# Hybrid SSM/attention layer with 32 experts: the mix product by column halves, earlier loads of x and the norm rows, and the b_down product moved to the 19th expert

## The chip, the cores and the metric

The kernel runs on one core of one Trainium2 chip. The metric is the device time in microseconds of one launch, as the median of several runs. The engines are named as in the profile: PE (TensorE, matrix products; PEld its weight loads), DVE (VectorE), ACT (ScalarE), POOL (GpSimd) and SP (SyncE, which here only issues DMAs). Each engine works through its own instructions in the order in which the program has them; semaphores make one wait for another.

## What is computed

One decoder layer for 256 tokens of width 1024, all in float32:

```python
proj   = x @ w_in                      # -> z, xBC, dt, q, k, v, gates
y_ssm  = mamba2_branch(z, xBC, dt) @ w_ssm_out       # 2048 x 1024
y_attn = sliding_window_attention(q, k, v) @ w_attn_out  # 1024 x 1024
merged = sigmoid(g0) * y_ssm + sigmoid(g1) * y_attn
h      = layer_norm(alpha * x + merged @ w_mix_out)
top_logits, top_idx = top_k(h @ w_router + b_router, 4)   # of 32 experts
gate_w = softmax(top_logits)
y_e    = swiglu(h @ w_gate_up[e] + b_gate_up[e]) @ w_down[e] + b_down[e]
out    = layer_norm(alpha * h + sum over the 4 of gate_w * y_e)
```

An expert's weights are 1024 x 2048 (gate/up) and 1024 x 1024 (down), 12 MiB; all 32 are read, 403 MB.

## The kernel before the change

**Front.** The weights of the front (w_in, w_attn_out, w_ssm_out, w_mix_out) come as a stream of 50 pieces of 1 MiB. SP loads piece i into one half of a pair of tiles, `ring`, which alternates (prefetch_raw, L101); a half is free again when piece i - 2 has been split. A split (split_ahead, L160) makes two fp32r tiles of a piece: ACT copies it (the high parts, L65), DVE subtracts the copy from it (the low parts, L68). A product then takes three matmuls in place of one: high by high, high by low, low by high (mm3, L332; mix, L826). Splits are made `la` pieces ahead; la is 1 here. Pieces 34 to 37 are w_attn_out (tile `ya`), 38 to 45 w_ssm_out (`yss`), 46 to 49 w_mix_out (`mix`). "Split 37" below is the split of piece 37, tile `w37` in the rows of the program's order.

**The pool.** `gran` has ten blocks of 16 KiB per partition. The ring, each split, large intermediate tiles (the attention output, the gated SSM output yt, the gates, the merged product m) and each piece of expert weights take one. A new tile is given a block when the program is built, and its first writer waits for the last user of the tile that had it.

**Attention and SSM product** (L762 to L819). Four steps of two 24-matmul groups on `ya`, then eight groups of 48 on `yss`, two for each of four output slices. Between them, PE turns the gated SSM output (L676), and ACT and DVE split what was turned. `later` and `run_due` put DVE and ACT work behind the group whose result it takes: for the SSM product a merge (mg, mrg, m: L782) with the gates. The loads of x, the two rows of the first norm, the router's weights (wr) and bias (br) are issued in the third of the four SSM steps (mix_loads, L789).

**Mix, norm, router** (L929 to L957). The mix product has two halves of tokens, c, and two of columns, and each half of columns takes two of the four pieces: mix(c, q). Before the change, c = 0 goes through all four q, then c = 1. resid adds x and takes the statistics of a half of columns; first_norm finishes a half of tokens; turn transposes it, logits multiplies it with the router, top finds the top four on DVE, place counts positions within each expert, one_hot makes the matrix that gathers an expert's tokens.

**Experts.** The work is a list of slots: for expert e eight "u" slots (gate/up) and then four "d" slots (down) of expert e - 1. Each block of 2 MiB serves two slots; SP issues block m when `prefetch` (L118) is reached for it in the program's order, in the mix and later up to nine blocks ahead of the slot (AH). `at(n, f)` puts f at slot n. residual(c) puts alpha * h into the accumulators `out` by a product with a scaled identity; residual(0) stands in the top-4 wait, residual(1) at slot 1. gates_down (L965) at slot 4 counts rows per expert, transposes the gate weights and has GpSimd load b_down; bias_down (L980) at slot 6 adds gate_w times b_down to the accumulators.

Of the kernel before, what the change touches and what calls it, by code (L numbers as in the profile page):

```python
# [8 lines left out]
F = mybir.dt.float32  # L9
# [6 lines left out]
P = 128  # L16
D = 1024
NT = 256
# [12 lines left out]
EXP_TANH = "exp_and_others"  # L31
SILU = "silu_and_others"
OVER, AL = 27, 7
DT, DD = 2, 4
D3 = 4
L1 = 1
# [7 lines left out]
def hybrid_layer(ctx, tc, x, w_in, conv_w, conv_b, dt_bias, a_log, d_skip, norm_w, w_ssm_out,  # L44
                 sinks, w_attn_out, b_gates, w_mix, ln1_g, ln1_b, w_router, b_router,
                 w_gate_up, b_gate_up, w_down, b_down, ln2_g, ln2_b, out, cap=CAP):
    nc = tc.nc
# [9 lines left out]
    def pair(name, dt=F):  # L57
        t = ptile(name, dt)
        return t[:, 0:2048], t[:, 2048:4096]

    def bank(name):
        return psum.tile([P, 512], F, name=name, tag="bank")

    def act(o, i, func=AF.Copy, **kw):
        return nc.scalar.activation(o, i, func, **kw)  # L65
# [12 lines left out]
    def mm(o, l, r, start, stop):  # L78
        return nc.tensor.matmul(o, l, r, start=start, stop=stop)  # L79

    def rows(ap, n, off=0):
        return bass.AP(tensor=ap.tensor, offset=ap.offset + off, ap=[[0, P], [1, n]])
# [5 lines left out]
    stream = []  # L88
# [9 lines left out]
    single = lone.tile([P, 2048], F, name="single")  # L98
    ring = pair("ring")

    def prefetch_raw():  # L101

        while st["dma"] < S_E:
            i = st["dma"]
            ap, nb = stream[i]
            if i - 2 >= st["split"]:
                break
            t = ring[i % 2]
            t3 = t.rearrange("p (k n) -> p k n", n=nb)
            nk = 2048 // nb // len(halves(i))  # L110
            for k in range(len(halves(i))):
                nc.sync.dma_start(t3[:, k * nk:k * nk + nk], ap[:, k * nk:k * nk + nk])
            raws[i] = t
            st["dma"] += 1

    moe = [0]

    def prefetch(upto):  # L118

        while moe[0] < min(upto, len(stream) - S_E):  # L120
            m = moe[0]
            ap, nb = stream[S_E + m]
            t = ptile(f"w{m}").rearrange("p (k n) -> p k n", n=nb)
            last = S_E + m == len(stream) - 1
            for ks in (slice(0, 2), slice(2, 3), slice(3, 4)) if last else (slice(0, 4096 // nb),):
                nc.sync.dma_start(t[:, ks], ap[:, ks])
            raws[S_E + m] = t
            moe[0] += 1

    def halves(i):  # L130

        return [slice(0, 1024), slice(1024, 2048)] if i == 0 else [slice(0, 2048)]
# [6 lines left out]
    def run_due():  # L139
        for t in sorted(t for t in due if t <= clock[0]):  # L140
            for fn in due.pop(t):
                fn()
# [72 lines left out]
    def w1(shape, name, dt=F):  # L215
        return work.tile(shape, dt, name=name, tag="w1", bufs=TB["w1"])
# [4 lines left out]
    def w4(shape, name):  # L221
        return work.tile(shape, F, name=name, tag="w4", bufs=TB["w4"])
# [119 lines left out]
    def take():  # L342
        nxt[0] += 1
        w = weights(nxt[0] - 1)
        if pend[0]:
            pend[0] = False
            side()
        return w
# [410 lines left out]
    bgn = bgn[0:32]  # L759
    nc.sync.dma_start(bgn, b_gate_up[0])  # L760
    mrg = mrg.rearrange("p (b t) -> p b t", t=NT)
    for n in range(4):  # L762
        hi, lo = take()
        for b in range(2):
            ps = bank(f"ya{n}{b}")[:, 0:NT]
            mm3(ps, hi, lo, slice(b * P, (b + 1) * P), att["h"], att["l"])
            later(1, lambda ps=ps, blk=2 * n + b: stt(mrg[:, blk], gts[1][:, blk], 1.0, ps, OP.add, OP.mult))
            tick(b == 1)
# [17 lines left out]
        act(mh[:, blk], mrg[:, blk], scale=0.5)  # L786
        stt(ml[:, blk], mrg[:, blk], 0.5, mh[:, blk].bitcast(F), OP.mult, OP.subtract)

    def mix_loads():  # L789
        xr = single.rearrange("p (c d) -> p c d", d=D)  # L790
        nc.sync.dma_start(xr, x[0].rearrange("(c p) d -> p c d", p=P))
        lnc = [w4([P, D], n) for n in ("lng", "lnb")]
        nc.sync.dma_start(lnc[0], rows(ln1_g, D))
        nc.sync.dma_start(lnc[1], rows(ln1_b, D))
        wr3 = w1([P, 8, 32], "wr")
        nc.sync.dma_start(wr3, w_router[0].rearrange("(k p) e -> p k e", p=P))
        br = w1([P, 32], "br")
        nc.sync.dma_start(br, rows(b_router, 32))
        return xr, lnc, wr3, br

    st["la"] = LS
    for n in range(4):
        prefetch((0, 1, 2, 2)[n])
        if n == 1:
            nc.scalar.preload_act_table_set(EXP_LN)
        if n == 2:
            xr, lnc, wr3, br = mix_loads()
        ps = [bank(f"yss{n}{b}")[:, 0:NT] for b in range(2)]
        for kh in range(2):
            hi, lo = take()  # L810
            if n == 3 and kh == 1:
                prefetch(3)
            for b in range(2):
                mm3(ps[b], hi, lo, slice(b * P, (b + 1) * P), *yT[kh], kh == 0, kh == 1)
                if kh:
                    later(1, lambda b=b, n=n, ps=ps: merge(2 * n + b, ps[b]))
                tick(b == 1)
            if n == 0 and kh == 0:
                bias_cols()  # L819
# [6 lines left out]
    def mix(c, q):  # L826
        hf, kh = divmod(q, 2)
        while len(wm) <= q:
            wm.append(take())
        hi, lo = wm[q]  # L830
        cs = slice(c * P, (c + 1) * P)
        for k in range(4):
            kk = 4 * kh + k
            mm(pm[c][hf], mh[:, kk, cs], hi[:, k], kk == 0, False)
            mm(pm[c][hf], mh[:, kk, cs], lo[:, k], False, False)
            mm(pm[c][hf], ml[:, kk, cs], hi[:, k], False, kk == 7)
# [3 lines left out]
    def resid(c, hf):  # L840
        hs = slice(512 * hf, 512 * hf + 512)
        stt(xr[:, c, hs], xr[:, c, hs], ALPHA, pm[c][hf], OP.mult, OP.add)
        nc.vector.bn_stats(bst[:, c, hf], xr[:, c, hs])
# [44 lines left out]
    def logits(c):  # L888
        pl[c] = bank(f"lg{c}")[:, 0:32]
        for k in range(8):  # L890
            mm(pl[c], hT[c][:, k], wr3[:, k], k == 0, k == 7)

    def top(c):
        tt(lg[:, c], pl[c], br, OP.add)
        nc.vector.max(t8[:, c], lg[:, c])
        ts(nm[:, c:c + 1], t8[:, c, 0:1], -1.0, None, OP.mult)
        nc.vector.memset(t8[:, c, 4:8], 3.0e38)
        nc.vector.match_replace(rp[:, c], t8[:, c], lg[:, c], -3.0e38)
        ts(mk[:, c], rp[:, c], -2.9e38, None, OP.is_le)
# [2 lines left out]
    G2 = const.tile([P, 2, 2, 64], F, name="G2")  # L902

    def place(c):
        if c:
            mm(pp[:, 1], ones, mk[:, 0], True, False)
        mm(pp[:, c], slt, mk[:, c], c == 0, True)
        stt(posm[:, c], pp[:, c], 1.0, mk[:, c], OP.add, OP.mult)
        ts(posm[:, c], posm[:, c], -1.0, None, OP.add)
# [10 lines left out]
    def residual(c):  # L920
        for hf in range(2):
            po[c][hf] = bank(f"out{c}{hf}")
            hs = slice(512 * hf, 512 * hf + 512)
            mm(po[c][hf], ia, hn[:, c, hs], True, False)

    def first_norm(c):
        norm(hn[:, c], [xr[:, c, 0:512], xr[:, c, 512:1024]], bst[:, c].rearrange("p a b -> p (a b)"), lnc, f"l1{c}")

    for q in range(4):  # L929
        mix(0, q)  # L930
        if q % 2:
            resid(0, q // 2)
        if q == 0:
            prefetch(4)
    mix(1, 0)
    first_norm(0)
    prefetch(5)
    mix(1, 1)
    resid(1, 0)
    prefetch(6)  # L940
    mix(1, 2)
    prefetch(7)
    mix(1, 3)
    resid(1, 1)
    prefetch(10)
# [6 lines left out]
    place(0)  # L952
    one_hot(0, 0)
    logits(1)
    top(1)
    place(1)
    one_hot(0, 1)  # L957
# [4 lines left out]

    gwT, bd = [], []

    def gates_down():  # L965

        mm(pp[:, 2], ones, mk[:, 0], True, False)
        mm(pp[:, 2], ones, mk[:, 1], False, True)
        nc.vector.tensor_reduce(cnt, pp[0:1, 2], op=OP.max, axis=AX.X)
        nc.vector.tensor_copy(cnti, cnt)  # L970
        pgt = bank("gwT")
        for c in range(2):
            nc.tensor.transpose(pgt[0:32, c * P:(c + 1) * P], gw[:, c], ident)
        gwT.append(mo.tile([P, NT], F, name="S", bufs=2))
        for hf in range(2):
            bd.append(mo.tile([P, 512], F, name="y", bufs=2))
            nc.gpsimd.dma_start(bd[hf][0:32], b_down[0, :, 512 * hf:512 * hf + 512])
        at(5, lambda: act(gwT[0][0:32], pgt[0:32, 0:NT]))

    def bias_down():  # L980
        for c in range(2):
            for hf in range(2):
                mm(po[c][hf], gwT[0][0:32, c * P:(c + 1) * P], bd[hf][0:32], False, False)

    front.close()

# [7 lines left out]
    def at(n, fn, pre=True):  # L994
        events.setdefault((n, pre), []).append(fn)
# [190 lines left out]

    gather(None, 0)
    at(0, lambda: (soft(0), soft(1), nc.scalar.preload_act_table_set(SILU)), pre=False)
    at(1, lambda: residual(1), pre=False)
    at(4, gates_down, pre=False)  # L1190
    at(6, bias_down, pre=False)
    cur = None
    for n, (kind, e, kp) in enumerate(slots):
        fire(n, True)
# [73 lines left out]
```

## Time and profile before

| | |
|---|---|
| median of 3 runs | 1339.33 us (1338.72 to 1339.79) |
| the profiled execution | 1339.34 us, its span 1337.6 us |
| mean granted TensorE clock | 0.98 |
| PE busy | 1252.5 us (94%) |
| DVE, ACT busy | 431.6 us (32%), 282.9 us (21%) |
| read from HBM | 461.11 MB, 346 GB/s over the span |

Times in the profile are microseconds from the first instruction. A row of the time line has start, duration, engine, line, operation, tiles (out<-in), shape, count, and in brackets how long the engine had stood and what ended that. A row of windows has the stretch, its length, then busy time and number of instructions for PE, PEld, DVE, ACT, POOL, then the granted clock, the share of the DMA engines and GB/s. A row of waits has the total, the number and the longest. A DMA issue row has count, size and the median time from issue to landing. A float32 product or a large one shows as two matmul records.

### The profile page before, as it was taken

The numbers are of one execution on the slowest core, as the hardware profiler recorded it, in microseconds if no ns is written. First come the engines' busy times: TensorE is split into PE (matmuls) and PEld (weight loads), VectorE is DVE, ScalarE is ACT, GpSimd is POOL, SyncE is SP. The second block draws the span as 40 slices with busy tenths as digits, with TensorE's granted clock in tenths as the row PEclk, the third lists the DMA queues.
The fourth block names the chain that finished last, engine by engine and source line by source line (L and its number), as shares of the span: only waits on it lengthen the run. The fifth ranks groups of instructions, "written<-read, shape, count | busy, mean of one in ns | idle before, by whom it ended". The sixth has DMA issues, their size and how long they took to land. (4 is left out here: it accounts for less than half of the span.)

```text
span 1337.6 us, 16127 instructions
## 1 busy us (share of the span) xinstructions
PE 1252.5 (94%) x6864; PEld 682.1 (51%) x6864; DVE 431.6 (32%) x816; ACT 282.9 (21%) x477; POOL 66.4 (5%) x37
## 2 busy tenths in 40 slices
PE   7998999999879999999999999898999999879985
PEld 7997878999754443433434434232333333233321
DVE  5999876565551211111121111111111121111113
ACT  4555545543311101100111011010101101001001
POOL 0045314000000000000000000000000000000000
PEclk9999989999988999999999999999999999989998
DMA  7543334657888999999999999999999999999994
GB/s 227 159 126 97 121 99 126 189 166 238 319 342 335 383 429 431 431 431 430 430 430 430 430 430 431 430 430 431 430 431 431 431 431 430 431 427 430 430 430 172
DMA packets 78741, 463.30 MB, mean 346 GB/s; under 512 B 6908, under 2 KB 45956, under 8 KB 53924
## 3 DMA queue, kind: packets, MB, share of 16 engines
q1 hardware_dynamic: 78452, 460.99, 84.6%
q8 instruction: 57, 0.93, 0.3%
q10 hardware_dynamic: 144, 1.05, 0.2%
q14 instruction: 24, 0.20, 0.0%
q0 software_dynamic: 64, 0.13, 0.0%
HBM read 461.11 MB, written 1.05 MB: 346 GB/s over the span
## 5 line engine op out<-in xcount | busy, mean ns | idle before, releaser
L79 PE MATMUL u<-w,xg 128*64 128x512 f32 x2048 | 464.5, 598 | 22.1 <-DMA w<-in_w_gate_up_dram 22.1
L79 PEld LDWEIGHTS u<-w,xg 128*64 128x64 f32 x2048 | 140.2, 137 | 314.7 <-issue 263.5
L79 PE MATMUL d<-w,ac 128*64 128x512 f32 x1024 | 241.1, 602 | 19.7 <-DVE gg L73 10.3
L1032 DVE COPY gu<-u 128x512 f32<-128x512 f32 x32 | 22.1, 691 | 682.9 <-PE u L79 682.9
L79 PE MATMUL ws<-x,w 128*128 128x256 f32 x1200 | 154.9, 289 | 2.8 <-ACT w L65 2.5
L79 PEld LDWEIGHTS ws<-x,w 128*128 128x128 f32 x1200 | 149.3, 195 | 6.1 <-ACT w L65 2.8
L79 PEld LDWEIGHTS d<-w,ac 128*64 128x64 f32 x1024 | 68.5, 137 | 142.3 <-issue 125.1
L68 DVE TENSOR_TENSOR w<-ring,w 128x2048 fp32r<-128x2048 f32 (+1 forms) x51 | 119.6, 2349 | 25.9 <-ACT w L65 25.7
L65 ACT ACTIVATE w<-ring 128x2048 fp32r<-128x2048 f32 (+1 forms) x51 | 95.8, 1878 | 76.0 <-DMA ring<-in_w_ssm_out_dram 13.1
L65 ACT ACTIVATE gu<-u 128x512 f32<-128x512 f32 x32 | 19.1, 597 | 318.3 <-PE u L79 318.3
L79 PEld LDWEIGHTS xg<-G,single 128*128 128x128 f32 x512 | 64.3, 200 | 24.9 <-issue 24.3
L79 PE MATMUL xg<-G,single 128*128 128x128 f32 x512 | 70.5, 292 | 0.2 <-DVE G L68 0.2
L79 PE MATMUL out<-y,S 64*128 64x512 f32 (+1 forms) x264 | 67.6, 616 | 0.8 <-ACT y L65 0.8
L65 ACT ACTIVATE xg<-xg 128x512 f32<-128x512 f32 x32 | 19.1, 597 | 219.5 <-PE xg L79 219.5
L65 ACT ACTIVATE hg<-hg 128x512 f32<-128x512 f32 x32 | 20.2, 631 | 153.0 <-DVE hg L72 153.0
L79 PE MATMUL yss<-yt,w 128*128 128x256 f32 x384 | 48.3, 288 | 4.0 <-ACT w L65 3.6
L79 PE MATMUL z<-w,x 128*128 128x512 f32 x192 | 50.3, 414 | 0.0
L79 PEld LDWEIGHTS yss<-yt,w 128*128 128x128 f32 x384 | 47.5, 196 | 4.6 <-ACT w L65 3.9
L1043 PEld LDWEIGHTS tu<-ident,gu 128*128 128x128 f32 x256 | 33.4, 210 | 26.3 <-issue 25.2
L79 PEld LDWEIGHTS out<-y,S 64*128 64x128 f32 (+1 forms) x264 | 23.4, 186 | 44.1 <-issue 42.5
L68 DVE TENSOR_TENSOR hg<-tu,bgu 128x256 f32<-128x256 f32 x64 | 26.8, 419 | 49.2 <-PE tu L1043 49.1
L79 PEld LDWEIGHTS z<-w,x 128*128 128x128 f32 x192 | 36.9, 196 | 10.1 <-issue 2.0
(213 smaller groups left out, 835.2 us busy)
## 6 DMA issues: line engine op xcount, KB each, us to landing
w<-in_w_gate_up_dram SPq DMA_DIRECT2D x128, 2048.0 KB, 38.4
w<-in_w_down_dram SPq DMA_DIRECT2D x63, 2048.0 KB, 38.8
ring<-in_w_in_dram SPq DMA_DIRECT2D x33, 1024.0 KB, 5.1
ring<-in_w_ssm_out_dram SPq DMA_DIRECT2D x8, 1024.0 KB, 5.3
ring<-in_w_attn_out_dram SPq DMA_DIRECT2D x4, 1024.0 KB, 5.1
ring<-in_w_mix_out_dram SPq DMA_DIRECT2D x4, 1024.0 KB, 7.2
single<-in_x_dram SPq DMA_DIRECT2D x2, 512.0 KB, 3.7
ring<-in_w_in_dram SPq DMA_DIRECT2D x2, 512.0 KB, 7.7
```

Of the source, the lines that this page charges most:

```text
L65: return nc.scalar.activation(o, i, func, **kw)
L68: return nc.vector.tensor_tensor(o, a, b, op=op)
L79: return nc.tensor.matmul(o, l, r, start=start, stop=stop)
L1032: nc.vector.tensor_copy(t, banks[hf])
L1043: nc.tensor.transpose(pb[:, b], gu[hf][:, b:b + 509:4], ident)
```

## The change

- **Loads.** x, norm rows, wr and br are issued ahead of the attention product, not in the SSM product. At its second step the last two pieces of w_mix_out (48 and 49) are loaded into a second ring pair (load_early), at the third step expert block 0 (prefetch(1)). Expert blocks 1 and on are issued from the mix on.
- **Splits.** When the SSM product is through, its last merge is put out, and then the splits of all w_mix_out pieces that remain (47 to 49).
- **Mix by column halves.** Both halves of tokens take columns 0 to 511 (pieces 46, 47), then both the rest (48, 49). first_norm(0) stands behind mix(1, 2).
- **Top-4 wait.** The count product `pos<-mk,ones` is taken out of place, and residual(1) is put between it and the second top-4.
- **b_down.** Slot 4 only counts rows. b_down is loaded as one tile 40 slots ahead of slot 220, the gates are transposed at slot 220, in the block of the 19th expert, and multiplied at slot 222.

```diff
+BIAS = 12 * 18 + 4
...
+    def load_early(*idx):
+        for i, t in zip(idx, pair("ring")):
+            early[i] = t
+            load_raw(i, t)
...
     nc.sync.dma_start(bgn, b_gate_up[0])
     mrg = mrg.rearrange("p (b t) -> p b t", t=NT)
+    xr = single.rearrange("p (c d) -> p c d", d=D)
+    nc.sync.dma_start(xr, x[0].rearrange("(c p) d -> p c d", p=P))
+    lnc = [w4([P, D], n) for n in ("lng", "lnb")]
+    nc.sync.dma_start(lnc[0], rows(ln1_g, D))
+    nc.sync.dma_start(lnc[1], rows(ln1_b, D))
+    wr3 = w1([P, 8, 32], "wr")
+    nc.sync.dma_start(wr3, w_router[0].rearrange("(k p) e -> p k e", p=P))
+    br = w1([P, 32], "br")
+    nc.sync.dma_start(br, rows(b_router, 32))
     for n in range(4):
+        if n == 1:
+            load_early(S_MIX + 2, S_MIX + 3)
+        if n == 2:
+            prefetch(1)
         hi, lo = take()
...
     for n in range(4):
-        prefetch((0, 1, 2, 2)[n])
         if n == 1:
             nc.scalar.preload_act_table_set(EXP_LN)
-        if n == 2:
-            xr, lnc, wr3, br = mix_loads()
...
             if n == 3 and kh == 1:
-                prefetch(3)
+                st["la"] = 2
...
     def place(c):
-        if c:
-            mm(pp[:, 1], ones, mk[:, 0], True, False)
         mm(pp[:, c], slt, mk[:, c], c == 0, True)
...
-    for q in range(4):
-        mix(0, q)
-        if q % 2:
-            resid(0, q // 2)
-        if q == 0:
-            prefetch(4)
+    run_due()
+    st["la"] = 4
+    split_ahead(S_MIX)
+    prefetch(3)
+    mix(0, 0)
+    prefetch(4)
+    mix(0, 1)
+    resid(0, 0)
+    prefetch(5)
     mix(1, 0)
-    first_norm(0)
-    prefetch(5)
+    prefetch(6)
     mix(1, 1)
     resid(1, 0)
-    prefetch(6)
+    prefetch(7)
+    mix(0, 2)
+    mix(0, 3)
+    resid(0, 1)
     mix(1, 2)
-    prefetch(7)
+    first_norm(0)
     mix(1, 3)
     resid(1, 1)
     prefetch(10)
...
     logits(1)
+    mm(pp[:, 1], ones, mk[:, 0], True, False)
+    residual(1)
     top(1)
...
-    at(1, lambda: residual(1), pre=False)
-    at(4, gates_down, pre=False)
-    at(6, bias_down, pre=False)
+    at(4, count_rows, pre=False)
+    at(BIAS - 40, load_bd, pre=False)
+    at(BIAS, lambda: gates_turned(BIAS), pre=False)
+    at(BIAS + 2, bias_down, pre=False)
```

How this moves instructions shows at three places. In the rows, numbers behind a name tell buffers apart; "waits" names the semaphores an instruction waits for, by the engine (or DMA queue) that raises them. The first is ACT in the attention product before the change: w36 to w38 are the copies of pieces 36 to 38, yt2 the turned SSM output.

```order
L65 ACTIVATE w36_2855<-ring_70 128x2048 [waits DMAHW0_49,DVE_49]
L65 ACTIVATE yt2_2799<-yt20_2860 128x4x128 [waits DVE_49,PE_49,Activation_49]
L65 ACTIVATE w37_2925<-ring_70 128x2048 [waits DMAHW5_49,DMAHW2_49,DVE_49]
L65 ACTIVATE yt2_2799<-yt21_2893 128x4x128 [waits PE_49]
L65 ACTIVATE w38_2988<-ring_70 128x2048 [waits DMAHW3_49,PE_49,Activation_49]
```

And the same place with the change:

```order
L66 ACTIVATE w36_2867<-ring_70 128x2048 [waits DVE_49,DMAHW0_49,PE_49,Activation_49]
L66 ACTIVATE yt2_2808<-yt20_2872 128x4x128 [waits DVE_49,PE_49,Activation_49]
L66 ACTIVATE w37_2939<-ring_70 128x2048 [waits DMAHW7_49,DVE_49,PE_49]
L66 ACTIVATE yt2_2808<-yt21_2905 128x4x128
L66 ACTIVATE w38_3002<-ring_70 128x2048 [waits DMAHW2_49,DVE_49,PE_49]
```

The order is the same, but the copies w36 and w37 now wait for PE too: w36 has the block of split 34, w37 that of split 36, and the semaphore count in the program is that of the last matmul that reads them.

The second place is PE from the mix to the first expert before the change: ht is the transposed h, lg the logits, pos the positions, xg the gathered tokens, u the gate/up product.

```order
L79 MATMUL mix00_3550<-w47_3569,m_3054 128x512 x12
L79 MATMUL mix01_3551<-w48_3592,m_3054 128x512 x12
L79 MATMUL mix01_3551<-w49_3609,m_3054 128x512 x12
L79 MATMUL mix10_3552<-w46_3491,m_3054 128x512 x12
...
L79 MATMUL pos_3567<-mk_3560,ones_3558 128x32
L79 MATMUL pos_3567<-mk_3560,slt_105 128x32
L79 MATMUL xg00_3815<-G2_3568,single_69 128x128 x8
```

With the change:

```order
L80 MATMUL mix00_3548<-w47_3572,m_3068 128x512 x12
L80 MATMUL mix10_3550<-w46_3492,m_3068 128x512 x12
L80 MATMUL mix10_3550<-w47_3572,m_3068 128x512 x12
L80 MATMUL mix01_3549<-w48_3574,m_3068 128x512 x12
...
L80 MATMUL pos_3565<-mk_3558,ones_3556 128x32
L80 MATMUL out10_3796<-single_69,ia_3555 128x512
L80 MATMUL out11_3798<-single_69,ia_3555 128x512
L80 MATMUL pos_3565<-mk_3558,slt_105 128x32
L80 MATMUL xg00_3820<-G2_3566,single_69 128x128 x8
```

The product of the second half of tokens with the first half of columns (mix10) stood behind all four groups of the first half of tokens, and now stands behind the first two of them; the residual product of the second half of tokens (out10, out11) has come in front of the second half's count product.

The third place is SP, which issues the loads, from the attention pieces on; before the change:

```order
L760 DMA mrg_2785<-in_b_gate_up_dram 32x2048
L112 DMA ring_70<-in_w_attn_out_dram 128x8x256
L112 DMA ring_70<-in_w_ssm_out_dram 128x8x256 x5
L126 DMA w0_3186<-in_w_gate_up_dram 128x4096
L112 DMA ring_70<-in_w_ssm_out_dram 128x8x256 x2
L126 DMA w1_3305<-in_w_gate_up_dram 128x4096
L791 DMA single_69<-in_x_dram 128x2x1024
L793 DMA lng_3308<-in_ln1_g_dram 128x1024
L794 DMA lnb_3309<-in_ln1_b_dram 128x1024
L796 DMA wr_3312<-in_w_router_dram 128x8x32
L798 DMA br_3314<-in_b_router_dram 128x32
L112 DMA ring_70<-in_w_ssm_out_dram 128x8x256
```

With the change:

```order
L771 DMA mrg_2785<-in_b_gate_up_dram 32x2048
L774 DMA single_69<-in_x_dram 128x2x1024
L776 DMA lng_2788<-in_ln1_g_dram 128x1024
L777 DMA lnb_2789<-in_ln1_b_dram 128x1024
L779 DMA wr_2792<-in_w_router_dram 128x8x32
L781 DMA br_2794<-in_b_router_dram 128x32
L109 DMA ring_70<-in_w_attn_out_dram 128x8x256
L109 DMA ring_2864<-in_w_mix_out_dram 128x4x512 x2
L109 DMA ring_70<-in_w_ssm_out_dram 128x8x256
L137 DMA w0_2937<-in_w_gate_up_dram 128x4096
L109 DMA ring_70<-in_w_ssm_out_dram 128x8x256 x7
L109 DMA ring_70<-in_w_mix_out_dram 128x4x512 x2
```

The five small loads stand ahead of the last attention piece, two mix pieces ahead of the first SSM piece, expert block 0 (here w0) behind that; block 1 has left this stretch.

More of the change, by code (lines that the diff above doesn't have):

```diff
@@ L99, in hybrid_layer, with load_raw @@
     ring = pair("ring")
+    early = {}
+    def load_raw(i, t):
+        ap, nb = stream[i]
+        t3 = t.rearrange("p (k n) -> p k n", n=nb)
+        nk = 2048 // nb // len(halves(i))
+        for k in range(len(halves(i))):
+            nc.sync.dma_start(t3[:, k * nk:k * nk + nk], ap[:, k * nk:k * nk + nk])
+        raws[i] = t
     def prefetch_raw():
@@ L104, in prefetch_raw @@
             i = st["dma"]
[L105 to L113, printed above, removed]
+            if i not in early:
+                if i - 2 >= st["split"]:
+                    break
+                load_raw(i, ring[i % 2])
             st["dma"] += 1
+    def load_early(*idx):
+        for i, t in zip(idx, pair("ring")):
+            early[i] = t
+            load_raw(i, t)
     moe = [0]
@@ L787, in merge @@
         stt(ml[:, blk], mrg[:, blk], 0.5, mh[:, blk].bitcast(F), OP.mult, OP.subtract)
[L789 to L799, printed above, removed]
     st["la"] = LS
     for n in range(4):
-        prefetch((0, 1, 2, 2)[n])
         if n == 1:
             nc.scalar.preload_act_table_set(EXP_LN)
-        if n == 2:
-            xr, lnc, wr3, br = mix_loads()
         ps = [bank(f"yss{n}{b}")[:, 0:NT] for b in range(2)]
@@ L963, in hybrid_layer, with count_rows @@
     gwT, bd = [], []
-    def gates_down():
+    def count_rows():
         mm(pp[:, 2], ones, mk[:, 0], True, False)
@@ L970, in gates_down, with load_bd, gates_turned @@
         nc.vector.tensor_copy(cnti, cnt)
+    def load_bd():
+        bd.append(mo.tile([32, D], F, name="bd", bufs=1))
+        nc.gpsimd.dma_start(bd[0], b_down[0])
+    def gates_turned(n):
         pgt = bank("gwT")
@@ L974, in gates_down @@
         gwT.append(mo.tile([P, NT], F, name="S", bufs=2))
[L975 to L978, printed above, removed]
+        at(n + 1, lambda: act(gwT[0][0:32], pgt[0:32, 0:NT]))
     def bias_down():
@@ L982, in bias_down @@
             for hf in range(2):
-                mm(po[c][hf], gwT[0][0:32, c * P:(c + 1) * P], bd[hf][0:32], False, False)
+                mm(po[c][hf], gwT[0][0:32, c * P:(c + 1) * P], bd[0][:, 512 * hf:512 * hf + 512], False, False)
     front.close()
```

## The prediction

> **What bounds the kernel now.** I read the page first, then the waits of the DMA-issuing queue, the windows around the start of the experts, and the instructions of TensorE in order of time from 280 to 470 us. The profiled execution took 1339.34 us: a span of 1337.6 and 1.74 around it. The median of the three runs is 1339.33, so no correction is needed between the two; 0.2%, 2.7 us, is about what a measurement can tell from no change.
>
> ```profile
> span 1337.6 us, 16127 instructions
> 404.90:460.20 55.30, 54.59 (x254) 25.21 (x256) 10.33 (x36) 7.30 (x13) 1.16 (x2) 0.92 0.90 344
> 460.20:1312.00 851.80, 809.97 (x3880) 309.02 (x3877) 125.73 (x330) 84.91 (x150) 0.30 (x1) 1.00 1.01 430
> ```
>
> The last three columns are granted clock, busy share of the DMA engines and GB/s. From 460 to 1312 us the expert weights arrive at 430 GB/s with the DMA engines full: a block of 2 MiB every 4.88 us, and nothing on an engine shortens that. What can move the end is the moment at which this stream becomes unbroken. In the 55 us before it ran at 344 GB/s, while TensorE was busy 54.59 of 55.30.
>
> ```profile
> SPq L126 <- PE u L79: 55.7, 8, 20.4
> 415.60 0.33 SPq L126 DMA_DIRECT2D w<-in_w_gate_up_dram  x1
> w<-in_w_gate_up_dram SPq DMA_DIRECT2D x1, 2048.0 KB, 7.8
> 450.40 0.33 SPq L126 DMA_DIRECT2D w<-in_w_gate_up_dram  x1
> w<-in_w_gate_up_dram SPq DMA_DIRECT2D x1, 2048.0 KB, 9.8
> ```
>
> The first row is of 410 to 460 us: the queue that issues expert blocks waits for the gate/up products to free a block. The pool holds ten, so block 10 goes out only when the products on block 0 end (415.60; it lands 7.8 us later), and block 16 at 450.40, landing at 460.2. From there on the stream is unbroken. So the end of the kernel hangs on when TensorE reaches the first expert, and on how fast it frees blocks 0 to 6. Both are sums over TensorE, below.
>
> ```profile
> 298.19 3.12 PE L79 MATMUL ya<-att,w 128*128 128x256 f32 x24
> 301.50 6.00 PE L79 MATMUL ya<-att,w 128*128 128x256 f32 x48
> 315.22 34.81 PE L79 MATMUL yss<-yt,w 128*128 128x256 f32 x288
> 353.68 2.57 PE L79 MATMUL yss<-yt,w 128*128 128x256 f32 x16 [3.65 <-ACT w L65]
> 356.65 4.96 PE L79 MATMUL yss<-yt,w 128*128 128x256 f32 x32 [0.40 <-DVE w L68]
> 361.44 3.13 PE L79 MATMUL mix<-w,m 128*128 128x512 f32 x13
> 366.74 5.58 PE L79 MATMUL mix<-w,m 128*128 128x512 f32 x23 [2.16 <-DVE w L68]
> 376.72 0.79 PE L79 MATMUL mix<-w,m 128*128 128x512 f32 x1 [4.40 <-ACT w L65]
> 379.05 15.31 PE L79 MATMUL mix<-w,m 128*128 128x512 f32 x59 [1.53 <-DVE w L68]
> 351.72 1.91 ACT L65 ACTIVATE w<-ring 128x2048 fp32r<-128x2048 f32 x1 [7.64 <-DMA ring<-in_w_ssm_out_dram]
> 333.06 11.51 SPq L798 DMA_DIRECT2D br<-in_b_router_dram  x1
> ```
>
> **Part by part: SSM product.** TensorE's 3.65 us wait stems from the x and norm loads: the last of them, br, held the issuing queue for 11.51 us, and the next weight piece left behind it, so that its copy waited until 351.72. The change sends these loads 50 us earlier. The wait goes, and with it the half-clock stretch that followed. Without both, the last 48 products take a sixth of the 34.81 us, 5.8, in place of 11.4 (350.03 to 361.44): 5.6 us off.
>
> **Attention product.** The loads land here, where a weight piece of 1 MiB is used every 6.0 us (48 products); what they cost DMA is hidden by that. But two blocks of the pool are now taken early (the second ring, expert block 0). The order of ScalarE shows split 37 waiting for TensorE: its block is that of split 36, free when the products on 36 end, 298.19 + 3.12 = 301.31.
>
> ```profile
> L65 ACT ACTIVATE w<-ring x20: 1901/1914/1918, 249.4 to 374.8; 128x2048 fp32r<-128x2048 f32 x20
> L68 DVE TENSOR_TENSOR w<-ring,w x20: 2281/2284/2293, 251.4 to 376.7; 128x2048 fp32r<-128x2048 f32 x20
> 301.78 0.60 ACT L65 ACTIVATE yt<-yt 128x512 fp32r<-128x512 f32 x1 [2.08 <-PE yt L676]
> 296.99 0.69 DVE L68 TENSOR_TENSOR yt<-yt,yt 128x512 fp32r<-128x512 f32 x1 [2.46 <-ACT yt L65]
> 361.65 0.42 DVE L76 SCALAR_TENSOR_TENSOR mg<-gate,yss 128x256 f32<-128x256 f32 x1 [0.82 <-PE yss L79]
> 362.10 0.42 DVE L68 TENSOR_TENSOR mrg<-mrg,mg 128x256 f32<-128x256 f32 x1
> ring<-in_w_attn_out_dram SPq DMA_DIRECT2D x4, 1024.0 KB, 5.1
> ring<-in_w_ssm_out_dram SPq DMA_DIRECT2D x1, 1024.0 KB, 6.9
> ```
>
> A copy takes 1.91 us, so the high parts come at 303.2 instead of 301.50: 1.7 us of standing. The low parts come later still: queued behind the copy is the turned piece yt on ScalarE (0.60), behind that its subtraction (0.69) and a merge (0.42) on VectorE, then the subtraction of the split, 2.28: 4.0 us, in which TensorE has 16 products of 0.125 us (48 in 6.00), 2.0. Another 2.0. I add 3.7; at best the second stall overlaps and it is 1.7, at worst a late piece adds the 1.8 by which the landing of the piece behind br (6.9 us, the last row) passes the median of the attention pieces.
>
> **Mix.** Now 32.9 us, 361.44 to 394.36. A product costs 0.24 us (13 in 3.13, 23 in 5.58), so 96 take 23.1; the rest is waiting for pieces that had not landed or not been split, and the clock. All four pieces are now in the chip by then. What is late next: the copy of the second piece stands on ScalarE behind the last merge. After the last SSM product come 0.2 us, two VectorE steps of 0.42, a copy of 0.42, then 1.91 and 2.28: low parts at 5.7 us, while TensorE has 13 products, 3.1. A stall of 2.6; the third and fourth splits are ready at 8.0 and 10.3, before they are used. 25.7 instead of 32.9: 7.2 off.
>
> **Clock.**
>
> ```profile
> 355.20:358.70 3.50, 3.10 (x15) 2.81 (x14) 3.50 (x2) 1.17 (x1) 0.00 (x0) 0.51 0.18 22
> 375.70:382.50 6.80, 4.24 (x9) 3.06 (x10) 2.29 (x1) 0.97 (x1) 0.00 (x0) 0.50 0.63 213
> 403.00:409.80 6.80, 5.77 (x26) 5.34 (x26) 1.66 (x10) 0.00 (x0) 1.16 (x2) 0.50 1.01 431
> 430.30:433.70 3.40, 3.40 (x10) 0.85 (x10) 0.00 (x0) 0.60 (x1) 0.00 (x0) 0.50 0.93 390
> ```
>
> Four stretches at half clock, two of 3.4 us and two of 6.8: one after the 3.65 us wait, one after 4.40, one in the top-4 wait, and one at 430 with TensorE busy 3.40 of 3.40. New stalls of about 2 us lie between; I count one stretch of 3.4, 1.7 us lost, with 0 and 3.4 as ends. The Trainium skill, "TensorE: Matmul & The Clock Gate" (Part 1), has the clock fall only after about 3.4 us of idling; by it this term would be 0 and the forecast 1.7 lower. The stretch at 430, with no idling in it, speaks against that.
>
> **Top-4 wait and first expert.**
>
> ```profile
> 403.96 0.61 PE L79 MATMUL pos<-mk,ones 128*128 128x32 f32 x2
> 405.37 0.64 PE L79 MATMUL pos<-mk,slt 128*128 128x32 f32 x2 [0.79 <-DVE mk L72]
> 411.90 3.65 PE L79 MATMUL u<-w,xg 128*64 128x512 f32 x16
> 415.49 1.98 PE L79 MATMUL out<-single,ia 128*128 128x512 f32 x4
> 423.17 0.38 PE L973 MATMUL gwT<-ident,gw 128*32 128x128 f32 x2
> 427.06 4.00 PE L79 MATMUL out<-y,S 32*128 32x512 f32 x8
> 431.00 4.99 PE L79 MATMUL u<-w,xg 128*64 128x512 f32 x16
> ```
>
> The residual product (1.98) now starts at about 404.5 and ends at 406.5; the count product behind it started at 405.37, so 1.1 is added (up to 3.1 if all of it runs at half clock). The first norm, moved a product later, ends about with the mix; 0.4 for that. Together 1.5. In return the first expert loses 1.98, about 0.3 (turning the gates), 4.0 (b_down), and the half clock in the 16 products at 431 (4.99 against 3.65: 1.3): 7.6 off.
>
> Sum. First expert product: 3.7 - 5.6 - 7.2 + 1.7 + 1.5 = 5.9 earlier, 406.0. Blocks from 3 on are freed 5.9 + 7.6 = 13.5 earlier. Block 10 goes out at 406.0 + 3.7 = 409.7 and lands at 417.5; blocks 1 to 9, issued as the mix proceeds from about 360, need 9 x 4.88 = 44 us and are in by about 406, so they don't bind. From 417.5 the stream can run at 4.88: block 16 would land at 446.8, and its issue (450.4 - 13.5 = 436.9, with 9.8 to land) allows it. I add 1.0, since with only two blocks under way the stream ran below 430 GB/s in the first window. 447.8 against 460.2: 12.4 earlier, and every later block with it.
>
> **b_down at the 19th expert.**
>
> ```profile
> PE u L79 <- DMA w<-in_w_gate_up_dram: 19.9, 23, 2.0
> w<-in_w_gate_up_dram SPq DMA_DIRECT2D x128, 2048.0 KB, 38.4
> ```
>
> The first row is of 600 to 1190 us: TensorE waits for weights about once an expert, so 4.3 us (6 with a half-clock stretch) are made up within some six experts. Until then the stream has 38.4 us of issued blocks: 0. Without that cover the 4.3 to 6 would be lost. The b_down load is as large as before.
>
> 1339.3 - 12.4 = 1326.9.
>
> **The rivals.**
> A: the new stalls do not halve the clock, the second attention stall overlaps: 3.4 less, 1323.5. For it: 2.16 us of waiting at 364.6 cost no clock. 0.18.
> B: the front gains nothing, only the first expert's 7.6 counts: 1339.3 - 7.6 + 1.0 = 1332.7. It needs 5.9 us more of waiting in the attention and SSM products: x, the norm rows and the router's 1024 rows of 128 bytes, behind which br held the queue for 11.51 us, now stand ahead of the last attention piece and the first SSM pieces. Against it: no product uses those pieces before 301, 20 us after the loads start. 0.17.
> C, slower: in the SSM product each split needs the block of the split two before, and the ring slot of the load two before: copy 1.91, subtraction 2.28, some 1.5 of queueing, load, within two groups of products, 11.6 us. A landing of up to about 5.9 us fits. At 10.3 each of four rounds loses 4.4, 17.6 in all: 1344.5. It decides from a landing of about 9.0 on, where four rounds eat the 12.4. Against it: after block 0 nothing else is in that queue. 0.03.
> D: no change: the blocks themselves come too late for an earlier stream. Blocks 1 to 16 would have to take from 362 to 460, 6.1 us each; that is the 344 GB/s of the first window, but there the queue was waiting for free blocks. 0.03.
>
> **Numbers.** The forecast (1324.5 to 1330) has 0.57; D and C 0.03 each; the 0.02 left are larger gains. The unknown terms (attention -2 to +1.8, clock +-1.7, count product +2, up to 5 us if the stream stays below 430 GB/s up to block 16) reach from 1322 to 1335; I give 1321.5 to 1334. Faster by over 0.2%: 0.94; within: 0.03; slower: 0.03.
>
> **What would show it.** Right: no wait behind br near 350; two waits of about 2 us near 301 to 307; a mix of about 26 us with one wait of 2 to 3; first expert product near 406; block 16 landing near 448, then 430 GB/s; no new wait of the issuing queue near the 19th expert. Wrong: a first expert product after 410, or gaps in the stream after 450.

## The result, and the profile after

The changed kernel takes 1324.48 us (median of 4 runs, 1324.27 to 1324.78) against 1339.28 for the kernel before in the same comparison: 14.8 us less, ratio 0.989 (95% interval 0.9873 to 0.9907). The forecast was 1326.9 with a range of 1321.5 to 1334. The profiled execution of the changed kernel took 1324.27 us, with a span of 1322.5, 15.1 shorter than before. The profiled execution of one experiment below (no_early, 1352.3 us) had a slower weight stream throughout (419 GB/s from 460 to 1290 us, where the others have 430), so a second run of that kernel gives its profile.

First the page's head and windows of the changed kernel: stretch, length, busy time and instructions of PE, PEld, DVE, ACT and POOL, then granted clock, share of the DMA engines, GB/s.

```profile
span 1322.5 us, 16117 instructions
361.10:364.50 3.40, 0.89 (x3) 0.19 (x1) 2.25 (x2) 3.40 (x3) 0.00 (x0) 1.00 0.82 328
364.50:367.90 3.40, 3.30 (x8) 2.66 (x9) 3.40 (x3) 1.32 (x1) 0.00 (x0) 0.50 1.06 451
395.20:398.60 3.40, 3.40 (x6) 1.34 (x6) 0.86 (x7) 0.00 (x0) 0.67 (x1) 0.50 0.95 405
404.90:460.20 55.30, 55.30 (x274) 21.77 (x272) 8.85 (x27) 5.61 (x9) 0.00 (x0) 1.00 0.98 410
406.00:412.00 6.00, 6.00 (x30) 1.87 (x26) 0.00 (x0) 0.00 (x0) 0.00 (x0) 1.00 0.70 240
445.00:1297.00 852.00, 812.92 (x3888) 310.20 (x3885) 125.74 (x330) 85.29 (x151) 0.29 (x1) 0.99 1.01 430
```

The stretch from 404.9 to 460.2, at 344 GB/s before, now runs at 410: one dent (406 to 412, 240 GB/s) is left of what was missing. The stream behind it is what it was, 430 GB/s. Of four half-clock stretches ahead of 445 us two are left, both of 3.4 us.

TensorE of the changed kernel in order of time (start, duration, operation, count, in brackets how long it had stood and for whom):

```profile
281.64 6.00 PE L80 MATMUL ya<-att,w 128*128 128x256 f32 x48
302.61 2.18 PE L80 MATMUL ya<-att,w 128*128 128x256 f32 x16 [1.56 <-ACT w L66]
306.35 4.09 PE L80 MATMUL ya<-att,w 128*128 128x256 f32 x32 [1.56 <-DVE w L69]
310.28 5.92 PE L80 MATMUL yss<-yt,w 128*128 128x256 f32 x48
318.16 40.57 PE L80 MATMUL yss<-yt,w 128*128 128x256 f32 x336
358.57 2.91 PE L80 MATMUL mix<-w,m 128*128 128x512 f32 x12
362.27 0.50 PE L80 MATMUL mix<-w,m 128*128 128x512 f32 x1 [0.79 <-ACT w L66]
364.60 20.68 PE L80 MATMUL mix<-w,m 128*128 128x512 f32 x83 [1.82 <-DVE w L69]
395.10 3.66 PE L80 MATMUL out<-single,ia 128*128 128x512 f32 x4
403.45 8.80 PE L80 MATMUL u<-w,xg 128*64 128x512 f32 x40
```

The same view of the kernel before, for the two borders that the prediction did not show:

```profile
282.33 6.00 PE L79 MATMUL ya<-att,w 128*128 128x256 f32 x48
307.34 2.92 PE L79 MATMUL yss<-yt,w 128*128 128x256 f32 x23
```

The two stalls of the attention product are there, one on the copy and one on the subtraction, 3.1 us together. The SSM product runs through: 336 products in 40.57 us without a wait. The mix waits once for the copy and once for the subtraction of its second piece, 2.61 together, and never for the third or the fourth. The first expert product starts at 403.45 instead of 411.90.

Issue of blocks 10 and 16 in the changed kernel's time line, and then each one's time from issue to landing:

```profile
407.15 0.33 SPq L137 DMA_DIRECT2D w<-in_w_gate_up_dram  x1
434.23 0.33 SPq L137 DMA_DIRECT2D w<-in_w_gate_up_dram  x1
```

```profile
w<-in_w_gate_up_dram SPq DMA_DIRECT2D x1, 2048.0 KB, 8.2
w<-in_w_gate_up_dram SPq DMA_DIRECT2D x1, 2048.0 KB, 10.9
```

Block 16 lands at 445.1; before it was 460.2. That is the 15.1 us by which the span is shorter, so nothing behind block 16 gained or lost.

### The profile page after: what moved, and what is told of

Read it like the earlier page. It is cut to its first block, busy times and chain, and to the rows that moved or that the text cites. A ratio compares the mean times of both kernels' runs of the same rounds, so it can differ in the third digit from the quotient of the medians.

```text
span 1322.5 us, 16117 instructions
## 1 busy us (share of the span) xinstructions
PE 1247.7 (94%) x6864; PEld 678.8 (51%) x6864; DVE 431.3 (33%) x816; ACT 282.6 (21%) x477; POOL 65.9 (5%) x36
## 5 line engine op out<-in xcount | busy, mean ns | idle before, releaser
L80 PE MATMUL out<-y,S 64*128 64x512 f32 x256 | 63.6, 615 | 0.8 <-ACT y L66 0.8
L80 PEld LDWEIGHTS out<-y,S 64*128 64x128 f32 x256 | 22.0, 186 | 41.9 <-issue 40.2
```

## The experiments

Twelve runs, in three groups. Executions of one kernel mostly spread over 1 to 9 us here (those of no_early over 30), so each median below stands with its ratio to the kernel before, measured beside it, and the ratio's 95% interval. The profiled executions of changed and variant kernels start the attention product, which no edit is meant to touch, anywhere from 280.46 to 282.40 us, so of a difference between absolute times in two profiles up to some 2 us can come from there.

**The changed kernel again.** No edit.

> The changed kernel itself once more, as a measure for the variants on the same chip. All theories: 14 to 15 us less than the kernel before, with 2 us of spread between executions; the half-clock stretches begin on a grid of 3.41 us, and how many of the stalls fill most of one cell of it changes from one execution to the next in steps of 1.7 us.

Measured: 1324.15 us (1322.05 to 1325.87), ratio 0.989 (0.9874 to 0.9907). This is the measure for what follows.

**The expert part undone.**

```diff
-    residual(1)
     top(1)
...
+    at(1, lambda: residual(1), pre=False)
     at(4, count_rows, pre=False)
-    at(BIAS - 40, load_bd, pre=False)
-    at(BIAS, lambda: gates_turned(BIAS), pre=False)
-    at(BIAS + 2, bias_down, pre=False)
+    at(4, load_bd, pre=False)
+    at(4, lambda: gates_turned(4), pre=False)
+    at(6, bias_down, pre=False)
```

> The changed kernel with the expert part undone: the second residual product at slot 1 again, b_down loaded, the gates transposed and multiplied at slots 4 to 6. Theory (TensorE's work in the first expert frees blocks later, and that moves the stream): the first expert product comes some 1.5 us earlier (402), the residual, the transposes, b_down and its half clock then hold blocks 3 and on 7.6 later, 6.1 net, so block 16 lands 5 us later, near 450, and the time is 1329.5 (1328 to 1331). Rival (after the change the DMA engines are full from about 363 on, so when blocks come free in the first expert no longer matters): block 16 near 445 as now, 1324.5 to 1325.5.

Measured: 1330.09 us, ratio 0.994 (0.9927 to 0.9954), some 6 us more than the changed kernel. TensorE (start of the attention product, first expert product), then issue and issue-to-landing time of block 16 in this run:

```profile
280.46 6.00 PE L80 MATMUL ya<-att,w 128*128 128x256 f32 x48
402.31 3.65 PE L80 MATMUL u<-w,xg 128*64 128x512 f32 x16
440.85 0.33 SPq L137 DMA_DIRECT2D w<-in_w_gate_up_dram  x1
```

```profile
w<-in_w_gate_up_dram SPq DMA_DIRECT2D x1, 2048.0 KB, 9.6
```

Block 16 is issued 6.6 us later and lands at 450.5, 5.3 later; counted from the start of the attention product, which comes 1.2 us earlier in this execution (280.46 against 281.64), that is 7.8 and 6.5. So the theory holds in what it says of the release: the slower release costs some 6 us once the front is no longer in the way. One part of it fails: the first expert product starts 1.1 us earlier, but all of that was there at the attention product, so taking the residual product out of the top-4 wait gained nothing. The half clock ran for 6.8 us there (394.6 to 401.4, granted clock 0.52), where it ran for 3.4 in the changed kernel.

**x, norm and router loads back in the SSM product.**

```diff
-    xr = single.rearrange("p (c d) -> p c d", d=D)
-    nc.sync.dma_start(xr, x[0].rearrange("(c p) d -> p c d", p=P))
...
-    nc.sync.dma_start(br, rows(b_router, 32))
...
     for n in range(4):
+        if n == 2:
+            xr = single.rearrange("p (c d) -> p c d", d=D)
+            nc.sync.dma_start(xr, x[0].rearrange("(c p) d -> p c d", p=P))
...
+            nc.sync.dma_start(br, rows(b_router, 32))
         if n == 1:
             nc.scalar.preload_act_table_set(EXP_LN)
```

> The changed kernel with x, norm rows, wr and br issued in the third SSM step again, all else as changed. Theory (the wait of 3.65 us and its half clock stem from these loads): a wait of 3 to 4 us near the seventh SSM piece returns, the SSM product takes 54 us in place of 48.3, everything behind moves by 5.6: 1330.1 (1329 to 1331.5). Rival (it was the expert block issued in the same step, no longer there, that made the piece late): no wait, 1324 to 1325.

Measured: 1323.1 us, ratio 0.9889 (0.9873 to 0.9904): no difference. The theory fell. The issuing queue and TensorE in this run:

```profile
335.82 5.35 SPq L815 DMA_DIRECT2D br<-in_b_router_dram  x1
341.28 0.38 SPq L109 DMA_DIRECT2D ring<-in_w_ssm_out_dram  x1
317.01 40.57 PE L80 MATMUL yss<-yt,w 128*128 128x256 f32 x336
```

br holds the queue for 5.35 us, not 11.51, the piece behind it goes out at 341.28 instead of 344.68, and TensorE never waits. What is missing from this queue against the kernel before is expert block 1, issued there at the head of the small loads. So both were put to the test on the kernel before, one at a time.

**On the kernel before: the small loads moved, nothing else; and block 1 kept out of the SSM product, nothing else.**

```diff
+    xr = single.rearrange("p (c d) -> p c d", d=D)
+    nc.sync.dma_start(xr, x[0].rearrange("(c p) d -> p c d", p=P))
...
+    nc.sync.dma_start(br, rows(b_router, 32))
...
-        if n == 2:
-            xr, lnc, wr3, br = mix_loads()
```

> The kernel before with only this of the change: x, norm rows, wr and br issued ahead of the attention product. Theory (the 3.65 us wait needs both the small loads and expert block 1 ahead of them in the same queue; taking either away is enough): no wait near 350, the attention product as long as before (25 us, no block is taken early), the mix with its own waits of 8 us as before: 5 us less than before, half-clock steps of 1.7 apart. Rival (expert block 1 alone makes the piece late): the wait stays, within 1 us of the kernel before.

```diff
-        prefetch((0, 1, 2, 2)[n])
+        prefetch((0, 1, 1, 1)[n])
```

> The kernel before with expert block 1 kept out of the SSM product (issued in the mix), x, norm rows, wr and br where they were. Theory (either is enough): br holds the queue for some 5.5 us in place of 11.5, the next piece lands in time and the wait near 350 goes; block 1 now loads beside the last mix pieces, which may cost 0 to 4 us there: 1.5 to 5.5 us less than before. Rival (the small loads alone make the piece late): the wait of 3 to 4 us stays, no less than before.

Measured: 1331.62 us, ratio 0.9951 (0.9936 to 0.9966), and 1336.45 us, ratio 0.9983 (0.9971 to 0.9995). TensorE in the first:

```profile
313.86 40.88 PE L79 MATMUL yss<-yt,w 128*128 128x256 f32 x336
368.74 0.50 PE L79 MATMUL mix<-w,m 128*128 128x512 f32 x1 [1.09 <-ACT w L65]
```

And in the second, with the issuing queue:

```profile
333.77 5.08 SPq L798 DMA_DIRECT2D br<-in_b_router_dram  x1
351.89 4.09 PE L79 MATMUL yss<-yt,w 128*128 128x256 f32 x32 [0.61 <-DVE w L68]
373.92 0.50 PE L79 MATMUL mix<-w,m 128*128 128x512 f32 x1 [3.76 <-ACT w L65]
```

The 3.65 us wait goes in both (0.61 is left in the second): either edit is enough, so the wait needs both, the 2 MiB of block 1 in flight and the small loads behind them. Moving only the loads is worth 6.9 us, as the mix pieces come earlier too (its wait for the last piece falls from 4.40 to 1.09). Moving only block 1 is worth 2.1. Its SSM product is 5.0 us shorter (49.15 against 54.10), but the mix is 3.7 longer (36.63 against 32.92). Block 1 now loads ahead of the last mix piece, whose copy starts 10.2 us after its issue (8.0 before), so 3.76 us of that wait stay and the mix waits 8.05 us in all, as before (8.09); and the half clock runs for 13.6 us of this mix instead of 6.8. The change does both, and one of them is then spare.

**Mix in its old order, early loads and splits kept.**

```diff
-    mix(1, 0)
-    prefetch(6)
-    mix(1, 1)
-    resid(1, 0)
-    prefetch(7)
     mix(0, 2)
+    prefetch(6)
     mix(0, 3)
     resid(0, 1)
+    prefetch(7)
+    mix(1, 0)
+    first_norm(0)
+    mix(1, 1)
+    resid(1, 0)
     mix(1, 2)
-    first_norm(0)
     mix(1, 3)
```

> The changed kernel with the mix in its old order, one half of tokens through all four pieces and then the other; the early loads and early splits stay. Theory (the mix is shorter because its pieces are loaded and split by then, not because of the order): third piece split at 8.0 and fourth at 10.3 us after the last SSM product, used at 8.3 and 11.2, so the mix stays at 26 to 27 us; pieces 46 and 47 give their blocks back 6 us later, a dent of about 1 us in the stream: 1324.5 to 1325.5. Rival (the order by columns is what makes the mix shorter, since the last two pieces are needed 24 products later): 4 to 6 us of waiting return in the mix, 1329 to 1330.5.

Measured: 1323.91 us, ratio 0.9894 (0.9877 to 0.991): no difference. TensorE in the mix:

```profile
362.73 0.49 PE L80 MATMUL mix<-w,m 128*128 128x512 f32 x1 [0.79 <-ACT w L66]
365.05 20.72 PE L80 MATMUL mix<-w,m 128*128 128x512 f32 x83 [1.83 <-DVE w L69]
```

The waits are those of the changed kernel to 0.01 us. With the pieces in the chip the order by columns adds nothing to the time.

**The order by columns kept, no early loads.** Run twice; the second run gives the profile.

```diff
-        if n == 1:
-            load_early(S_MIX + 2, S_MIX + 3)
...
-                st["la"] = 2
+                st["la"] = 1
...
-    run_due()
-    st["la"] = 4
-    split_ahead(S_MIX)
-    prefetch(3)
...
```

Expert blocks 1 to 6 are then issued one or two groups of the mix later.

> The changed kernel without the second ring pair: w_mix_out pieces 48 and 49 come through the ring as before, splits one piece ahead, the expert blocks behind them; the order by column halves, the early x loads, the top-4 wait and b_down as changed. Split 37 finds a block of the pool then. Both theories: the two stalls of the attention product go (3.1 us), and the mix waits little (0 to 2 us), since by columns its last piece is needed only after 60 of 96 products, 17 us behind the last SSM product, and is split by 15.6. Theory 1 (the end now hangs on the DMA engines, full from about 363 on: 2 MiB of mix pieces and a start of the blocks some 5 us later are not made up): block 16 lands 2 us later, 2 us more than the changed kernel. Theory 2 (it hangs on when TensorE reaches the first expert and frees blocks): 3 us less than the changed kernel.

> The kernel without the second ring pair once more, for its times and for a profile. Theory 1 (the DMA engines set the end once TensorE is early enough): first expert product near 398, 5 to 6 us earlier than with the second pair, yet blocks 1 to 16 land one behind the other without a gap from about 365 on, block 16 within 2 us of 445, and the time is within 1.5 us of the changed kernel. Theory 2 (TensorE sets it): block 16 near 440, 5 us less.

Measured: 1324.88 us, ratio 0.99 (0.9878 to 0.9923), with executions scattered from 1322.3 to 1340.2 beside the one named above; and again, 1323.85 us (1323.5 to 1325.38), ratio 0.9899 (0.988 to 0.9919): no difference from the changed kernel, neither 2 us more nor 3 us less. TensorE and block 16's issue in the second run:

```profile
301.34 6.00 PE L80 MATMUL ya<-att,w 128*128 128x256 f32 x48
359.72 11.17 PE L80 MATMUL mix<-w,m 128*128 128x512 f32 x48 [1.11 <-DVE w L69]
371.65 8.24 PE L80 MATMUL mix<-w,m 128*128 128x512 f32 x35 [0.75 <-DVE w L69]
400.73 8.80 PE L80 MATMUL u<-w,xg 128*64 128x512 f32 x40
431.51 0.33 SPq L137 DMA_DIRECT2D w<-in_w_gate_up_dram  x1
```

Its windows, and blocks 10 and 16 from issue to landing:

```profile
389.00:399.20 10.20, 9.96 (x35) 7.60 (x35) 1.66 (x10) 0.58 (x1) 0.67 (x1) 0.50 1.02 418
404.00:445.00 41.00, 41.00 (x208) 16.99 (x204) 8.18 (x22) 4.63 (x8) 0.00 (x0) 1.00 1.00 429
```

```profile
w<-in_w_gate_up_dram SPq DMA_DIRECT2D x1, 2048.0 KB, 11.0
w<-in_w_gate_up_dram SPq DMA_DIRECT2D x1, 2048.0 KB, 13.0
```

The attention product has no stall, the mix waits 1.86 us in all, and the first expert product starts at 400.73, 2.7 us earlier than in the changed kernel. Block 10 goes out 2.7 us earlier (404.42), but lands at 415.4 as there (407.15 + 8.2 = 415.35), because the blocks ahead of it are still arriving: from 404 to 445 the engines are full at 429 GB/s, without the dent. Block 16 goes out 2.7 us earlier as well (431.51), takes 13.0 us in place of 10.9 and lands at 444.5, 0.6 earlier. So here the DMA engines, not the release of blocks, set when the blocks land. (The 10.2 us at half clock ahead of the first expert cost TensorE some 5.1, an estimate from the granted clock of 0.50. As an earlier first expert product gains next to nothing at the end, this loss should not show there either; no run tests it.)

**Expert block 0 one attention step later.**

```diff
-        if n == 2:
+        if n == 3:
             prefetch(1)
```

> The changed kernel with expert block 0 issued one attention step later, at the fourth in place of the third. In the program's order split 37 then no longer waits for TensorE, since it finds a block of the pool. Theory (that wait made the two stalls of 1.56 us in the attention product): both go, all behind them is 3 us earlier, 1321.4 (1321 to 1322). Rival 1 (the end is set by the DMA stream's start, which does not move): 1324 to 1325. Rival 2 (block 0 now loads beside the first SSM pieces and makes one late): the stall comes back in the SSM product, 1324 to 1327.

Measured: 1323.36 us (1320.33 to 1324.07), ratio 0.9881 (0.9863 to 0.9899); no difference that can be told. TensorE and, from windows, the clock of the profiled execution (the slowest of the four):

```profile
302.07 4.10 PE L80 MATMUL ya<-att,w 128*128 128x256 f32 x32 [0.26 <-DVE w L69]
328.12 27.14 PE L80 MATMUL yss<-yt,w 128*128 128x256 f32 x224 [0.54 <-DVE w L69]
361.12 21.85 PE L80 MATMUL mix<-w,m 128*128 128x512 f32 x83 [1.83 <-DVE w L69]
402.78 8.80 PE L80 MATMUL u<-w,xg 128*64 128x512 f32 x40
```

```profile
360.25:367.05 6.80, 5.93 (x14) 4.67 (x15) 6.02 (x5) 2.09 (x2) 0.00 (x0) 0.50 1.00 425
391.00:397.80 6.80, 6.80 (x22) 4.98 (x22) 1.64 (x10) 0.00 (x0) 0.67 (x1) 0.50 1.01 431
```

The first stall goes and 0.26 of the second is left, so what the prediction said of the block of split 37 is shown. But 0.54 comes back in the SSM product, and the half clock runs for 6.8 us twice, where it ran for 3.4 twice: 3.4 us lost again, by an estimate from the granted clock of 0.50. Counted from the start of the attention product (280.49 here), the first expert product comes no earlier than in the changed kernel (122.3 against 121.8 us). That the clock is what hides the gain in the median is argued from this one profile, not shown.

**The b_down product: left out, and at the end.**

```diff
-    at(BIAS, lambda: gates_turned(BIAS), pre=False)
-    at(BIAS + 2, bias_down, pre=False)
```

> The changed kernel without the transposed gates and without the b_down product at the 19th expert (the load of b_down stays): the part gate_w times b_down is missing from the output. Theory (the 4.3 us of products there are covered by TensorE's waits for weights in the following experts, and the issued blocks carry the stream): within 0.5 us of the changed kernel, 1323.6 to 1324.7. Rival (they delay the stream for good): 4 us less, near 1320.

```diff
-BIAS = 12 * 18 + 4
+BIAS = 12 * 31 + 8
```

> The changed kernel with the transposed gates at slot 380 and the b_down product at slot 382, within the last two products of the program, in place of slots 220 and 222. Theory (the product is free only while TensorE still has waits for weights ahead of it): after slot 382 only some 1 to 1.6 us of waiting is left, so most of the 4.3 us shows: 2.5 to 4.5 us more than the changed kernel, 1326.7 to 1328.7. Rival (place does not matter, the last block's landing sets the end): no more than 1 us more.

Measured: 1323.38 us, ratio 0.9897 (0.9877 to 0.9917), the same; and 1328.67 us, ratio 0.9934 (0.9913 to 0.9955), 4.5 us more than the changed kernel and 5.3 more than the variant without the product, measured beside it. The end of TensorE's work in the second:

```profile
1306.18 3.69 PE L80 MATMUL out<-bd,S 32*128 32x512 f32 x8
1312.44 1.99 PE L80 MATMUL out<-y,S 64*128 64x512 f32 x8 [0.70 <-ACT y L66]
```

and of the changed kernel:

```profile
1307.39 1.99 PE L80 MATMUL out<-y,S 64*128 64x512 f32 x8 [0.76 <-ACT y L66]
```

The last wait is there with and without the product (0.70 and 0.76), so it covers nothing. The last products come 5.0 us later; 1.0 of that was there when the last block landed, the rest is the b_down product's 3.69 and the transposes in front of it (0.39). At the 19th expert the work is free, at the end it is paid in full: the cover that the prediction named is real.

**Both causes of stalls treated.** Block 0 a step later, and the copy of piece 47 ahead of the last merge on ScalarE.

```diff
-        if n == 2:
+        if n == 3:
             prefetch(1)
...
-    run_due()
+    st["la"] = 1
+    split_ahead(S_MIX)
     st["la"] = 4
     split_ahead(S_MIX)
```

> The changed kernel with expert block 0 issued at the fourth attention step and, behind the SSM product, the copy of piece 47 put ahead of the last merge on ScalarE (its subtraction behind the merge's steps on VectorE). Theory 1 (both TensorE and the DMA stream behind the SSM product start some 2.5 us earlier, and the stalls of 0.79 and 1.82 us at the start of the mix, which cost a half-clock stretch too, shrink to about 1): the first expert product comes 4 to 6 us earlier, the gap in the stream before block 10 closes, 3 to 5 us less than the changed kernel, 1319 to 1321. Rival (the half clock takes it back as it did with block 0 moved alone): within 1.5 us of the changed kernel.

Measured: 1321.38 us (1319.71 to 1322.41), ratio 0.9873 (0.9851 to 0.9895). It is the lowest median of all, 2.8 us below the changed kernel, but the intervals overlap, so the lead is not settled. TensorE:

```profile
356.88 3.13 PE L80 MATMUL mix<-w,m 128*128 128x512 f32 x13
361.63 19.11 PE L80 MATMUL mix<-w,m 128*128 128x512 f32 x83 [1.61 <-DVE w L69]
```

The wait for the copy goes, 1.61 for the subtraction stays, and 83 products take 19.11 us where they took 20.68, at full clock. Ahead of the first expert the half clock runs longer than in the changed kernel:

```profile
389.80:400.00 10.20, 9.96 (x35) 7.60 (x35) 1.65 (x10) 0.41 (x1) 0.67 (x1) 0.50 0.99 406
```

Ten microseconds of it instead of 3.4 take back some 3.4 us of TensorE, so the first expert product (401.59) comes 1.9 us earlier, or 2.6 counted from the start of the attention product (282.36), and not 4 to 6. The first expert block behind the SSM product goes out earlier too, at 357.84 instead of 359.53, so both limits move, the release of blocks and the start of the stream; how much of the 2.8 us each is worth is not shown.

## Why the prediction was right, and where it was not

The path and the signs were right, and one cause was not. Term by term, with the start of each stage as border:

| term | forecast, us | measured, us |
|---|---|---|
| attention product (28.64 against 25.01) | +3.7 | +3.6 |
| SSM product (48.29 against 54.10) | -5.6 | -5.8 |
| mix and its clock (26.71 against 32.92) | -7.2 + 1.7 | -6.2 |
| mix's end to first expert product (18.17 against 17.54) | +1.5 | +0.6 |
| start of the attention product (281.64 against 282.33) | 0 | -0.7 |
| first expert product | -5.9 | -8.45 |
| release in the first expert (issues of block 10 and of block 16) | -7.6 | -7.7 |
| stream up to block 16 (measured: its issue to landing, 10.9 against 9.8) | +1.0 | +1.1 |
| block 16 lands | -12.4 | -15.1 |

**The sizes.** 2.7 us lie between forecast and profile. 0.7 are in front of the change: the profiled executions of the variants, which share that stretch, start the attention product anywhere from 280.46 to 282.40. 0.9 are the top-4 wait, and come of two misses that partly cancel. The second half's count product came 2.3 us later behind the end of the mix (13.27 against 11.01 us), not 1.5, since the residual product ran at half clock and took 3.66 where the forecast had 1.98. But from there to the first expert product it took 4.90 us instead of 6.53, since the 6.8 us of half clock had become 3.4 and were over; the forecast left them as they were. 0.7 are the mix. Its stall was forecast as 2.6 and measured as 2.61, and the one half-clock stretch of 3.4 us came right behind it; the products themselves were taken a little too long. The last term's agreement is partly luck, for the two numbers are not the same thing: from the landing of block 10 to that of block 16, where the forecast put its 1.0, it took 29.8 us, 0.5 more than six blocks at 4.88.

**The step that failed: what made the 3.65 us wait.** The prediction put it on x and the norm loads alone. loads_back shows that with these loads in their old place, and block 1 gone from there, nothing is lost; b_x_early and b_w1_late show that either edit alone removes the wait. The size of the term was right because the change makes both, which the prediction did not rely on: luck, as far as the cause goes. Read alone, br's row of 11.51 us names the instruction that stood, not the 2 MiB ahead of it that were moving.

**The step that held only just: "they don't bind".** Blocks 1 to 9 were to be in the chip by about 406. Block 9's row in the changed kernel (issued at 385.68):

```profile
w<-in_w_down_dram SPq DMA_DIRECT2D x1, 2048.0 KB, 22.8
```

It lands at 408.5, after block 10 is issued (407.15). Two limits have nearly met: TensorE's release of blocks (exp_back: 6.6 us later there is 5.3 us later at block 16) and the DMA engines, full from 364 on (no_early_again: 2.7 us earlier on TensorE is 0.6 earlier at block 16). Three parts of the change can be undone one at a time at no cost, and mostly for another reason, that two parts cure one wait: the small loads and block 1 in the SSM product; the early pieces and the order by columns in the mix, where either alone leaves 2.6 or 1.9 us of waiting and b_x_early, which has neither, waits 5.4. What no_early gains on TensorE beyond that, the DMA engines take.

**Rivals.** B needed 5.9 us more of waiting in the attention and SSM products than forecast; the attention product waited 3.1 where 3.7 were forecast, the SSM product not at all. C needed landings of over 9 us for the SSM pieces; the seven issued from 306 us on landed in 4.9 to 7.0. D is out with 410 GB/s in the first window. A gave nearly the right time for the wrong reason: the two attention stalls did not overlap, and the clock was lost.

## What to carry to other kernels

When a wait ends on a transfer, ask what was moving in the queue ahead of it, and take the suspects away one at a time: two edits that each cure the same stall look like two gains and are worth one. When a front stage feeds a stream that then runs at the rate of the DMA engines, count both limits, when the compute releases buffers and when the stream could have been full; past the point where they meet, an earlier release buys next to nothing. Work of a few microseconds was free in the middle of a stretch where the engine waits once a round for weights, and was paid in full behind the last of those waits.

## What the runs showed of the hardware

**The granted clock goes by a grid.** Read in steps of 0.85 us, the four half-clock stretches of the kernel before start at 355.2, 375.7, 403.0 and 430.3: 20.5, 27.3 and 27.3 apart, which is 6, 8 and 8 times 3.41. All last one or two such cells (three in no_early_again and in best). The Trainium skill, "TensorE: Matmul & The Clock Gate" (Part 1), describes a free-running window of 3.41 us, and here the trace agrees. It has the clock fall after a window of idling; there the trace says more: the window 361.1 to 364.5 above, with TensorE busy 0.89 of 3.40, was enough, while two attention stalls of 1.56 us, each within a cell of its own (busy 1.85 and 1.84 of 3.41), cost no clock. The kernel before narrows it down: its cell from 348.4 to 351.8, busy 1.63 of 3.40, cost nothing, and the next, busy 1.52, was followed by half clock at 355.2. Busy time alone does not decide, for ahead of the stretch at 430 that the prediction shows the cell was full, in the kernel before:

```profile
426.90:430.30 3.40, 3.40 (x10) 1.40 (x8) 0.00 (x0) 0.00 (x0) 0.00 (x0) 1.00 0.92 318
```

What filled it was the b_down product (427.06 to 431.06), with 32 rows where the others have 64 or 128. The same product at the 19th expert of the changed kernel (912.35, 3.69 us) brought no half clock (granted 1.00 from 907 to 924). What the clock counts is not settled by these runs.

**A small load can hold the queue for long.** br, 128 rows of 32 numbers behind wr's many small rows, held the issuing queue for 11.51 us behind a block of 2 MiB and for 5.1 to 5.6 without one; the weight piece behind it went out only then.
